# Score priority, a whole-bank output norm, and conditioning products moved to GpSimd and ScalarE in a hybrid decoder trunk

## The chip, the core and the metric

The kernel runs on one core of a Trainium2 chip. A core has five engines with queues of their own: TensorE (PE; its weight loads are listed as PEld), VectorE (DVE), ScalarE (ACT), GpSimd (POOL) and SyncE (SP), which here issues nearly all DMA. Each engine works through its instructions in the order fixed when the kernel was built; semaphores hold an instruction until its operands are there. Matmuls read SBUF and write PSUM, which has eight banks of 128 x 512 float32. The metric is the device time of one execution in microseconds (us), lower is better; the times given are medians over several executions.

## The reference

Two decoder layers on one sequence of 256 tokens of width 1024. A layer has three sub-layers: a half-step SwiGLU FFN, a token mixer, another half-step FFN. Layer 0 mixes with an HGRN2 gated linear recurrence (8 heads, 128 x 128 state, chunks of 64 tokens), layer 1 with a chunked gMLP. Every sub-layer is wrapped in the same way, with shift, scale and gate from a conditioning vector `c`:

```python
cond = jax.nn.silu(c)
mod = (cond @ ada_w[i] + ada_b[i]).reshape(B, 3 * N_SUB, D_MODEL)[:, :, None, :]

def sublayer(x, fn, pre_g, post_g, shift, scale, gate, res_w):
    h = rms_norm(x, pre_g) * (1.0 + scale) + shift
    return x + res_w * gate * rms_norm(fn(h), post_g)
```

The recurrence, per head and chunk (`bb` is the running sum of the log of the forget gate):

```python
o_inter = jnp.einsum('bhtk,bhkv->bhtv', qb * jnp.exp(bb), state)
decay = jnp.exp(jnp.where(causal, diff, -jnp.inf))     # diff = bb[t] - bb[s]
scores = jnp.einsum('bhtk,bhtsk,bhsk->bhts', qb, decay, kb)
o_intra = jnp.einsum('bhts,bhsv->bhtv', scores, vb)
...
o = rms_norm(o, out_norm) * gate        # per head, over 128 values
return o.reshape(B, S, D_MODEL).astype(h.dtype) @ w_out
```

## The kernel before

**Matmuls in three products.** Inputs, weights and results are float32. Each operand is split into a high part in a reduced float32 format and a low part, and a product is made of three matmuls: high x high, high x low, low x high (`mm3`, `mm3f`, `chunk2`; lines 160, 441, 431).

**Weights.** All weights come from HBM once, as a list of blocks of 128 x 2048 float32 in the order of use. A block is brought in as two halves: `cast` (L113) loads a 512 KB half into one of four raw buffers (tile `raw`) and casts it on ScalarE to the high part (L122); `sub` (L129) subtracts on VectorE for the low part (L132). Both parts lie in tiles of a pool of 14 (`wtile`), so at most seven blocks are in SBUF, fewer where the recurrence keeps its own tensors there. `next_block` (L148) hands out the next ready block and makes new ones until `ahead` are in store.

**Conditioning.** The 144 columns of `cond @ ada_w` are not matmuls: each is a 128 x 1024 tile (512 KB) that VectorE multiplies with `cond` and sums along the free axis in one instruction (`ada`, L179; the instruction at L192). Three tiles (`adap`) hold loads in flight; the load of a later one is issued on SyncE's queue when an earlier one is worked off. They are spread over the work as background: `pace(upto, blocks)` sets up to which column the next `blocks` weight blocks bring it, and `wblock` (L141) does so many after each block. The limits per sub-layer are in `bgs` (L1111). `pre_cols` (L197) and `gate_tile` (L212) make the pre-norm columns and the gate row `G` out of them, and first make any column that is still missing.

**Order of the work.** Outside the boundaries a planner orders the instructions of each engine before the run, by priority: a smaller place in the program goes first, when its operands are there by the planner's own estimate. `self.gate` and `hold` add fixed orders to it. Loads on SyncE keep program order.

**Boundary** (`boundary`, L297). Between two sub-layers the order on ScalarE, VectorE and TensorE is written out by hand. There are two token tiles t of 128 and two halves h of 512 columns. For a tile: the last matmuls of the output, `mm(t, h)`; the square and its sum per half (`square`, L235); `gated` (L310), the product with `G`; `half_mean` (L242) and `inv_rms` (L247); `residual` (L251), which adds into `x` and squares the new `x`; `scaled` (L290), the normalised `xn`; then per half four transposes on TensorE (L271), four ScalarE instructions for the high part of `h` (L274), four on VectorE for the same value in float32 (L284) and one difference for the low part (L287). `halves(n)`, `cast` and `sub` between these steps bring in weights for the next sub-layer. The first projection of the next sub-layer (`proj`, L400; matmuls at L412) is laid around the second tile's steps: `p0`, its 48 matmuls for tile 0, is cut after 30 and after 36 of them. In `p0` the 17th to 20th need the low part of half 0, the 21st to 24th that of half 1.

**Recurrence** (`hgrn`, L627). Eight heads in two halves of four (`hb`). `feat` makes features on the partitions, `tok` tokens on the partitions, `gate_f` (L666) the forget gate's logs and exponentials on ScalarE and VectorE. `attn` (L693) is a generator: scores are built in seven levels (64, 32, ... 1); at each, VectorE takes differences (L724, L729), ScalarE the exponential (L80), VectorE a product (L735), TensorE 16 matmuls of 64 columns (L741), and VectorE merges the result of the level before by a mask (L712). At the end the output products (L774, L776) go to PSUM. `zip_steps` alternates a step of `attn` with a step of other matmul work, so that TensorE has something to do. `finish` (L781) is the output norm: eight squares with sums on ScalarE (L787), the reciprocal root, eight scale-and-gate instructions on VectorE (L800), eight transposes (L805), and the split into high and low (L809, L810). For `hb` 0 it runs inside the steps of the second half's `attn`, followed by the output projection of its two pairs of heads (`outs`, L884: two times eight calls of `out_mm`, three matmuls each); for `hb` 1 it stands alone at the end, ahead of the boundary.

## Time and profile before

| | us |
|---|---|
| median of 3 executions | 1200.78 (1199.64 to 1204.22) |
| profiled execution | 1199.71 |
| its span, first to last instruction | 1197.9 |
| TensorE busy | 1144.4 (96%) |
| VectorE busy | 909.9 (76%) |
| ScalarE busy | 663.3 (55%) |
| GpSimd busy | 6.8 (1%) |

The page gives one profiled execution. In a timeline row stand the start, the duration, the engine, the line of the kernel, the operation, output and inputs by the names of their tiles, shapes and count; a bracket at the end is the time that the engine stood idle before it and what ended that. In a row of groups, the number after `x` is the count, then busy time and mean duration in nanoseconds, then idle time before the group with those that ended it. A row of windows gives the busy time of each engine inside a stretch, with counts, the clock granted to TensorE (1.00 is full), the share of time that the DMA engines were busy, and GB/s.

The sub-layers follow one another like this, by the transposes of the boundaries (L271): boundary 0, from the first FFN to the recurrence, around 213 us; boundary 1 around 397 to 413; boundary 2 around 587 to 601; boundary 3, into the gMLP, until about 790; boundary 4 around 1013; the last FFN to the end.

### The profile page before, as it was taken

Reading aid. Unit: us, or ns where it says so; the run is one execution under the profiler, and the core shown is the slowest. Engines: PE = TensorE matmul, PEld = TensorE weight load, DVE = VectorE, ACT = ScalarE, POOL = GpSimd, SP = SyncE. Lnnn points to the kernel's source line nnn. Section 1 sums busy time; section 2 is a strip of 40 time slices with the busy share of each in tenths; the row PEclk is TensorE's granted clock in tenths of the full one; section 3 lists DMA queues with packets and bytes.
Section 4 is the critical chain, followed back from the end, with each engine's and each line's share of the span. In section 5 each row is a group of like instructions: output and inputs, shape, how many; then the busy total and the mean of one; then the engine's idle time right before and its main releaser. Section 6 shows DMA issues by size and latency. Waiting matters only on the chain.

```text
span 1197.9 us, 17119 instructions
## 1 busy us (share of the span) xinstructions
PE 1144.4 (96%) x6518; PEld 997.4 (83%) x6518; DVE 909.9 (76%) x1391; ACT 663.3 (55%) x1054; POOL 6.8 (1%) x16
## 2 busy tenths in 40 slices
PE   7999998898798899999999999999999999999997
PEld 6989997798787688888788888877798997888886
DVE  6987786779867789985589986476898777866642
ACT  6454446668547755555565555553664456645531
POOL 0000000000000000000000000000000000000000
PEclk9999999898899999999999999999999999999999
DMA  9889898296305389986279996426687764766630
GB/s 349 311 315 331 320 351 287 95 327 233 125 35 193 106 293 365 333 307 224 94 261 339 344 334 227 165 80 222 234 316 276 265 201 131 247 216 226 207 106 36
DMA packets 79764, 282.31 MB, mean 236 GB/s; under 512 B 9873, under 2 KB 10561, under 8 KB 79682
## 3 DMA queue, kind: packets, MB, share of 16 engines
q1 hardware_dynamic: 78626, 278.05, 66.0%
q0 software_dynamic: 1056, 3.17, 0.8%
q8 instruction: 51, 0.84, 0.3%
q14 instruction: 31, 0.25, 0.1%
HBM read 280.11 MB, written 1.07 MB: 235 GB/s over the span
## 4 chain that ended last, share of the span: by engine, by line
PE 83%; DVE 8%; DMA 4%; ACT 4%; issue 1%; SPq 0%; DVEq 0%; ACTq 0%
PE ups L437 17%; PE ups L438 9%; PE y L162 8%; PE y L163 8%; PE y L164 8%; PE pps L412 7%; PE ups L557 4%; PE ups L445 4%; PE ups L443 4%; PE ups L444 4%; DVE w L132 2%; PE ab L741 2%; DMA raw<-in_wffn 2%; ACT w L122 1%; PE vps L1003 1%
## 5 line engine op out<-in xcount | busy, mean ns | idle before, releaser
L132 DVE TENSOR_TENSOR w<-raw,w 128x1024 fp32r<-128x1024 f32 x376 | 453.8, 1223 | 113.5 <-ACT w L122 105.5
L122 ACT CAST w<-raw 128x1024 fp32r<-128x1024 f32 x376 | 387.1, 1050 | 167.7 <-DMA raw<-in_wffn 66.0
L437 PE MATMUL ups<-h,w 128*128 128x512 f32 x864 | 302.0, 393 | 0.0
L438 PE MATMUL ups<-h,w 128*128 128x256 f32 x864 | 242.0, 280 | 0.0
L437 PEld LDWEIGHTS ups<-h,w 128*128 128x128 f32 x864 | 161.7, 187 | 36.4
L192 DVE CUSTOM_DVE_ANT_0 ada<-ada,cond 128x1024 f32<-128x1024 f32 x144 | 173.6, 1221 | 21.7 <-DMA ada<-in_ada 21.7
L162 PE MATMUL y<-w,t 128*128 128x512 f32 x448 | 179.7, 402 | 0.0
L163 PE MATMUL y<-w,t 128*128 128x512 f32 x448 | 178.2, 398 | 0.3 <-DVE w L132 0.3
L164 PE MATMUL y<-w,t 128*128 128x512 f32 x448 | 177.7, 397 | 0.0
L438 PEld LDWEIGHTS ups<-h,w 128*128 128x128 f32 x864 | 163.3, 189 | 1.0
L445 PE MATMUL ups<-h,w 128*128 128x256 f32 x416 | 117.9, 283 | 2.1 <-DVE rs_sd L89 1.2
L443 PE MATMUL ups<-h,w 128*128 128x256 f32 x416 | 118.3, 284 | 0.0
L444 PE MATMUL ups<-h,w 128*128 128x256 f32 x416 | 117.7, 283 | 0.0
L412 PE MATMUL pps<-w,h 128*128 128x512 f32 x480 | 115.1, 396 | 0.2 <-DVE h L287 0.2
L412 PEld LDWEIGHTS pps<-w,h 128*128 128x128 f32 x480 | 89.9, 190 | 19.2 <-DVE h L287 0.6
L164 PEld LDWEIGHTS y<-w,t 128*128 128x128 f32 x448 | 84.6, 189 | 20.3
L162 PEld LDWEIGHTS y<-w,t 128*128 128x128 f32 x448 | 84.7, 189 | 18.9
L163 PEld LDWEIGHTS y<-w,t 128*128 128x128 f32 x448 | 84.7, 189 | 18.9 <-DVE w L132 1.4
L445 PEld LDWEIGHTS ups<-h,w 128*128 128x128 f32 x416 | 79.7, 191 | 2.5 <-DVE w L132 2.5
L443 PEld LDWEIGHTS ups<-h,w 128*128 128x128 f32 x416 | 79.7, 192 | 1.0 <-issue 0.2
L444 PEld LDWEIGHTS ups<-h,w 128*128 128x128 f32 x416 | 79.7, 192 | 0.8 <-issue 0.2
L80 ACT ACTIVATE t<-t 128x256 f32<-128x256 f32 (+2 forms) x70 | 36.6, 524 | 50.4 <-DVE t L490 41.7
(196 smaller groups left out, 1327.1 us busy)
## 6 DMA issues: line engine op xcount, KB each, us to landing
raw<-in_wffn SPq DMA_DIRECT2D x264, 512.0 KB, 5.5
ada<-in_ada SPq DMA_DIRECT2D x144, 512.0 KB, 6.7
raw<-in_wgmu SPq DMA_DIRECT2D x48, 512.0 KB, 5.0
raw<-in_whg SPq DMA_DIRECT2D x40, 512.0 KB, 5.2
raw<-in_wgmv SPq DMA_DIRECT2D x24, 512.0 KB, 5.0
G<-gflat POOLq DMA_DIRECT2D x6, 512.0 KB, 5.1
t<-in_gbin SPq DMA_DIRECT2D x6, 256.0 KB, 5.6
x<-in_x SPq DMA_DIRECT2D x2, 512.0 KB, 4.3
```

The source lines that it names most:

```text
L122: self.after(self.nc.scalar.copy(hi[:, sl], raw), self.hold[0])
L132: self.after(self.nc.vector.tensor_sub(lo[:, sl], raw, hi[:, sl]), self.hold[1])
L162: self.paced(mm(ps, l[0], r[0], start=start, stop=False))
L163: mm(ps, l[0], r[1], start=False, stop=False)
L164: mm(ps, l[1], r[0], start=False, stop=stop)
L192: self.after(nc.vector.tensor_tensor_reduce(t, t, self.cond, 1.0, 0.0, ALU.mult, ALU.add, self.mod[i // 24][:, i % 24:i % 24 + 1]), self.h ...
L412: lambda g=g, i=i, j=j, kc=kc, w=w: mm(res[g][t], h2[:, i, t, kc, :], w, start=kc + i + j == 0, stop=i == 1 and kc == KC - 1)))
L437: self.paced(mm(ps, u[0], self.h2[:, :, :, kc, :], start=kc == 0, stop=False))
L438: self.last = mm(ps[:, 1, :], u[1], self.h2[:, 0, :, kc, :], start=False, stop=kc == KC - 1)
L443: self.paced(mm(o, u[0], h[0], start=start, stop=False))
L444: mm(o, u[0], h[1], start=False, stop=False)
L445: self.last = mm(o, u[1], h[0], start=False, stop=stop)
```

## The change

- **Conditioning in the recurrence** (`ada`): while `self.pooled` is set, a product is a `tensor_mul` on GpSimd, in place, and its sum a ScalarE `activation` (Copy) with an accumulated output. It is set in `hgrn` from the start to just before its end.
- **Pace**: the first FFN's limit goes from 46 to 40 columns, the recurrence (limit 64) spreads its own over 14 blocks, not 9, and the third FFN's limit goes from 118 to 120.
- **Priority**: each step of `attn` is built 400 places ahead in the planner's priority.
- **Output norm**: squares of a whole bank into SBUF, sums and the gating product on VectorE by whole banks, then eight scalings of 128 x 128. At the end of the recurrence it is written out by hand in the boundary's region, opened earlier for that; the output projection of the second pair of heads (24 matmuls, `fill`) is taken out of the alternation and laid between its steps.
- **Boundaries**: `half_mean` of the residual comes after both halves; for half 1 of tile 0 the float32 value of `h` is made on ScalarE ahead of the residual, and its difference on VectorE after it; the projection is built after that; `p0` is cut at 35 and 41; the weight half in the midst of this goes to the end of the boundary. Boundary 1 has its own numbers of weight halves.
- **gMLP**: the gate row is made at unit 8 of 12, not before the units; three small constants are loaded at the start of the kernel.

```diff
@@ ada
-            self.after(nc.vector.tensor_tensor_reduce(t, t, self.cond, 1.0, 0.0, ALU.mult, ALU.add,
-                                                      self.mod[i // 24][:, i % 24:i % 24 + 1]), self.hold[1])
+            m = self.mod[i // 24][:, i % 24:i % 24 + 1]
+            if self.pooled:
+                nc.gpsimd.tensor_mul(t, t, self.cond)
+                self.after(nc.scalar.activation(t, t, AF.Copy, accum_out=m), self.hold[0])
+            else:
+                self.after(nc.vector.tensor_tensor_reduce(t, t, self.cond, 1.0, 0.0, ALU.mult, ALU.add, m),
+                           self.hold[1])
@@ residual
                 self.square(self.x[t][:, hs], st[0], h)
-                if h == 0:
-                    self.half_mean(st)
+        if st is not None:
+            self.half_mean(st)
@@ h_low becomes h_full and h_low
+    def h_full(self, h, pa, cols, scalar=False):
...
+            if scalar:
+                nc.scalar.activation(hf[:, ks], pa[:, ks], AF.Identity, bias=sh[:, kc:kc + 1], scale=A[:, kc:kc + 1])
+            else:
+                nc.vector.tensor_scalar(hf[:, ks], pa[:, ks], A[:, kc:kc + 1], sh[:, kc:kc + 1],
+                                        op0=ALU.mult, op1=ALU.add)
+        return hf
@@ boundary
+    def boundary(self, y, G, mm, cols, table, plan=(4, 2, 0, 0)):
...
-        self.halves(4)
+        self.halves(plan[0])
...
-        self.halves(2)
+        self.halves(plan[1])
...
+        for _ in range(plan[2]):
+            self.cast()
         self.residual(0, yg, r, sx)
+        for _ in range(plan[2]):
+            self.sub()
...
-        self.h_low(0, 0, pa0, cols)
-        self.h_low(0, 1, pa1, cols)
-        w = [[self.ready.pop(0) for _ in range(2)] for _ in range(2)]
-        self.res, go = self.proj(w)
+        self.h_low(0, 0, self.h_full(0, pa0, cols))
         sq(1, 1, sy1)
         gated(1, 1, yg1)
         r = self.inv_rms(sy1)
-        self.cast()
+        for _ in range(plan[3]):
+            self.cast()
+        hf = self.h_full(1, pa1, cols, scalar=True)
         self.residual(1, yg1, r, sx1)
-        self.sub()
+        for _ in range(plan[3]):
+            self.sub()
+        self.h_low(0, 1, hf)
+        w = [[self.ready.pop(0) for _ in range(2)] for _ in range(2)]
+        self.res, go = self.proj(w)
...
-        do(p0[0:30])
+        do(p0[0:35])
         pa0, _ = self.h_high(1, 0, xn, cols)
-        do(p0[30:36])
+        do(p0[35:41])
         pa1, act = self.h_high(1, 1, xn, cols)
-        do(p0[36:])
-        self.h_low(1, 0, pa0, cols)
-        dve = self.h_low(1, 1, pa1, cols)
+        do(p0[41:])
+        self.h_low(1, 0, self.h_full(0, pa0, cols))
+        dve = self.h_low(1, 1, self.h_full(1, pa1, cols))
+        self.halves(1)
@@ hgrn
-        self.pace(bg, 9)
+        self.pace(bg, 14)
+        self.pooled = True
...
+        def attn(hb, bank, res):
+            gen = attn_steps(hb, bank, res)
+            while True:
+                with tc.high_priority(offset=400):
+                    if next(gen, gen) is gen:
+                        return
+                yield
...
+        def stats(hb, ops, sqrt):
...
+            for u in range(2):
+                sqs.append(self.t2().rearrange("p (i v) -> p i v", i=4))
+                nc.scalar.activation(sqs[u], ops[u].rearrange("p t h v -> p (t h) v"), AF.Square)
+            def gated(u):
+                c0 = 2 * (2 * hb + u) * P
+                nc.vector.tensor_mul(og[:, 512 * u:512 * u + 512].rearrange("p (t c) -> p t c", t=NT),
+                                     ops[u].rearrange("p t h v -> p t (h v)"), gg[:, :, c0:c0 + 2 * P])
+            for u in range(2):
+                nc.vector.reduce_sum(ss[:, 4 * u:4 * u + 4], sqs[u], axis=mybir.AxisListType.X)
+                if u == 0:
+                    gated(0)
             nc.vector.tensor_scalar(ss, ss, 1.0 / P, EPS, op0=ALU.mult, op1=ALU.add)
             if sqrt:
                 self.tact(ss, ss, AF.Sqrt)
+                self.cast()
+                gated(1)
                 nc.vector.reciprocal(r, ss)
...
+        def turn(hb, u, og, r):
...
+                nc.vector.tensor_scalar(on[:, i, :], on[:, i, :], r[:, 4 * u + i:4 * u + i + 1], None, op0=ALU.mult)
...
-        finish(1, ops[1], True)
+        self.ahead, self.pooled = 0, False
+        fill = products(1)
         wos = [nb()]
         self.ahead = 1
         wos.append(nb())
+        self.open()
+        self.gate = state["ops"]
+        for op in fill[:5]:
+            op()
+        og, r = stats(1, ops[1], True)
+        ps = [turn(1, 0, og, r)]
+        fill[5]()
+        ps.append(turn(1, 1, og, r))
+        self.sub()
+        for op in fill[6:]:
+            op()
+        for u in range(2):
+            split(1, u, ps[u])
         nxt(y, G, self.out_last(y, oTs[2:], wos))
@@ gmlp: G = G_fn() moves from before the units to
+            if u == 8:
+                G = G_fn()
@@ run
-        bgs = {"ffn0": 46, "hg": 64, "ffn1": 92, "ffn2": 118, "gm": 138, "ffn3": 144}
+        bgs = {"ffn0": 40, "hg": 64, "ffn1": 92, "ffn2": 120, "gm": 138, "ffn3": 144}
...
+                    self.boundary(y, G, mm, st["cols"], tables[subs[s + 1][0]], (2, 1, 1, 1) if s == 1 else (4, 2, 0, 0))
```

More of the change, by code (lines that the diff above doesn't have):

```diff
@@ L775, in attn @@
                                              start=True, stop=False)
-                        nc.tensor.matmul(ops[:, t, hd, :], St[:, hl * S + t * P:hl * S + (t + 1) * P],
-                                         v[:, t, c0:c0 + P], start=t == 0, stop=True)
+                        state["ops"] = nc.tensor.matmul(
+                            ops[:, t, hd, :], St[:, hl * S + t * P:hl * S + (t + 1) * P],
+                            v[:, t, c0:c0 + P], start=t == 0, stop=True)
                 res.append(ops)
@@ L779, in attn @@
             yield
-        def finish(hb, ops, sqrt=False):
+        def attn(hb, bank, res):
[6 more added lines that the diff above has]
+        def stats(hb, ops, sqrt):
             ss = self.tiny.tile([P, 8], F32, tag="ss8", name="ss8")
-            o4 = [o.rearrange("p t h v -> p (t h) v") for o in ops]
+            r = self.tiny.tile([P, 8], F32, tag="r8", name="r8")
+            og, sqs = self.t4(), []
@@ L784, in finish @@
             for u in range(2):
-                for i in range(4):
-                    junk = self.scr.tile([P, 512], BF16, tag="junka", name="junka")
-                    nc.scalar.activation(junk[:, 0:P], o4[u][:, i, :], AF.Square, accum_out=ss[:, 4 * u + i:4 * u + i + 1])
+                sqs.append(self.t2().rearrange("p (i v) -> p i v", i=4))
[4 more added lines that the diff above has]
+                                     ops[u].rearrange("p t h v -> p t (h v)"), gg[:, :, c0:c0 + 2 * P])
@@ L793, in finish @@
             else:
+                gated(1)
                 self.rsqrt(r, ss)
[L795 to L811 removed]
@@ new lines, in stats @@
+            return og, r
+        def turn(hb, u, og, r):
+            on = og[:, 512 * u:512 * u + 512].rearrange("p (i v) -> p i v", i=4)
+            for i in range(4):
+                nc.vector.tensor_scalar(on[:, i, :], on[:, i, :], r[:, 4 * u + i:4 * u + i + 1], None, op0=ALU.mult)
+            ps = self.acc.tile([P, 512], F32, tag="acc", name="ots")
+            for i in range(4):
+                c0 = (i % 2) * S + (i // 2) * P
+                nc.tensor.transpose(ps[:, c0:c0 + P], on[:, i, :], self.ident)
+            return ps
@@ L813, in hgrn, with split @@
+        def split(hb, u, ps):
+            pair = 2 * hb + u
+            if not oall:
+                oall.extend([self.wtile() for _ in range(2)])
+            oT = [o[:, 512 * pair:512 * pair + 512] for o in oall]
+            nc.scalar.activation(oT[0], ps, AF.Copy, scale=self.onorm)
+            nc.vector.scalar_tensor_tensor(oT[1], ps, self.onorm, oT[0], op0=ALU.mult, op1=ALU.subtract)
+            oTs.append([o.rearrange("p (h s) -> p h s", h=2) for o in oT])
         ybank = {"i": 0}
@@ L1102, in run @@
         self.blocks, self.blk, self.ready, self.ahead = [], 0, [], 0
-        self.half, self.casts, self.hold = None, [], (None, None)
+        self.half, self.casts, self.hold, self.pooled = None, [], (None, None), False
         for src, n, k in ((d["wffn"][0], 2048, 33), (d["whg"], 2048, 20), (d["wffn"][1], 2048, 33),
```

63 lines of the change are left out of this document (21 added, 42 removed).

## The prediction

> **What bounds the kernel now.** I read the page first, then the order of time on TensorE for places where it stands still, then busy time by stretch, and last what the other engines did ahead of each stop.
>
> ```profile
> PE 1144.4 (96%) x6518; PEld 997.4 (83%) x6518; DVE 909.9 (76%) x1391; ACT 663.3 (55%) x1054; POOL 6.8 (1%) x16
> PE 83%; DVE 8%; DMA 4%; ACT 4%; issue 1%; SPq 0%; DVEq 0%; ACTq 0%
> ```
>
> TensorE is busy in 1144.4 of 1197.9 us and carries 83% of the chain that ended last. Nothing in the diff removes a matmul, so all that can be won is TensorE's idle time, some 53 us, and the slow clock that follows a long stop. The timeline of TensorE shows the stops (the bracket is the idle time and what ended it):
>
> ```profile
> 213.51 0.47 PE L271 MATMUL npa<-ident,xn 128*128 128x128 f32 x1 [8.09 <-DVE be L242]
> 289.17 0.45 PE L741 MATMUL ab<-t 128*128 128x64 f32 x1 [5.09 <-ACT L L679]
> 314.67 0.45 PE L741 MATMUL ab<-t 128*128 128x64 f32 x1 [6.64 <-DVE t L735]
> 382.51 0.90 PE L805 MATMUL ots<-ident,t 128*128 128x128 f32 x3 [4.95 <-DVE t L800]
> 397.48 0.33 PE L271 MATMUL npa<-ident,xn 128*128 128x128 f32 x1 [1.56 <-DVE be L242]
> 409.07 0.33 PE L271 MATMUL npa<-ident,xn 128*128 128x128 f32 x1 [2.41 <-DVE xn L293]
> 598.80 0.33 PE L271 MATMUL npa<-ident,xn 128*128 128x128 f32 x1 [1.57 <-DVE xn L293]
> 787.40 0.33 PE L271 MATMUL npa<-ident,xn 128*128 128x128 f32 x1 [1.98 <-DVE xn L293]
> 837.79 0.27 PE L219 MATMUL gps<-ident,gate 128*8 128x128 f32 x1 [1.15 <-DVE w L924]
> 838.93 0.50 PE L163 MATMUL pps<-w,h 128*128 128x512 f32 x1 [0.86 <-DVE w L132]
> 854.16 0.39 PE L445 MATMUL ups<-h,w 128*128 128x256 f32 x1 [0.93 <-DVE w L132]
> 1012.76 0.33 PE L271 MATMUL npa<-ident,xn 128*128 128x128 f32 x1 [1.56 <-DVE xn L293]
> ```
>
> L271 is the transpose in a boundary between two sub-layers (five of them: I count from 0), L741 the recurrence's scores, L805 its output's transposes, L219 and L163 lie in the gMLP. After a long stop the clock is down as well; the 16 score matmuls of one level, once after the stop at 289 and once in full flow (columns: stretch, its length, TensorE busy, weight loads busy, granted clock, DMA share, GB/s):
>
> ```profile
> 289.10:292.90 3.80, 3.65 (x16) 3.49 (x16) 0.50 0.29 116
> 298.60:300.60 2.00, 1.89 (x16) 1.82 (x16) 1.00 0.03 8
> ```
>
> 3.65 against 1.89: a stop of 5 us or more costs 1.76 us on top. Those under 2 us show no such loss: I price them at their length.
>
> **Boundary 0 (the FFN into the recurrence).** The wait at 213.51 names a DVE row, but the delay starts on ScalarE:
>
> ```profile
> 204.65 1.05 ACT L122 CAST w<-raw 128x1024 fp32r<-128x1024 f32 x1 [1.93 <-DMA raw<-in_whg]
> 206.22 1.05 ACT L122 CAST w<-raw 128x1024 fp32r<-128x1024 f32 x1 [0.52 <-DMA raw<-in_whg]
> 207.17 0.59 ACT L235 ACTIVATE junka<-y 128x512 bf16<-128x512 f32 x1
> ```
>
> Two weight casts, written into the order ahead of the square of the second half, wait for their loads. TensorE's last matmul before the stop ended at 213.51 - 8.09 = 205.4; the 27 between (18 of mm(1,0), 9 of mm(1,1)) at 0.23 us each put the end of mm(0,1) at about 199. The square at 207.17 is 8 us late, and the chain behind it, 6.3 us to 213.51, is shorter than the cover. What makes the loads late is the first FFN's traffic:
>
> ```profile
> 150.00:180.00 30.00, 30.00 (x207) 27.72 (x206) 25.02 (x35) 12.63 (x16) 1.22 (x2) 1.00 0.97 351
> ...
> ada<-in_ada SPq DMA_DIRECT2D x144, 512.0 KB, 6.7
> ```
>
> With a DMA share of 0.97 at 351 GB/s the stream is DMA's. The limit of conditioning products in this FFN goes from 46 to 40: six loads of 512 KB fewer, 3.15 MB / 351 GB/s = 9.0 us of stream. That is about the lateness, so the stop should nearly go: of 8.09 + 1.76 = 9.85 I take 7.5. Bounds: 0 (the stream holds back elsewhere, in the four raw buffers) and 9.85. If the loads come, next is the chain itself.
>
> **Boundaries 2, 3 and 4.** ScalarE and VectorE in boundary 2 ahead of the stop at 598.80, and the matmuls that cover it:
>
> ```profile
> 590.24 2.46 PE L412 MATMUL pps<-w,h 128*128 128x512 f32 x10
> ...
> 591.63 1.04 ACT L122 CAST w<-raw 128x1024 fp32r<-128x1024 f32 x1
> ...
> 591.65 1.37 DVE L284 TENSOR_SCALAR hf<-npa,A,shift 128x128 f32<-128x128 f32 x4
> 593.66 0.68 DVE L310 TENSOR_TENSOR yg<-y,G 128x512 f32<-128x512 f32 x1
> 596.00 0.15 DVE L242 TENSOR_SCALAR be<-s 128x1 f32<-128x1 f32 x1 [0.79 <-ACT junka L235]
> ```
>
> The product L310 could run at 591.6, when ScalarE's square is over, but stands behind four scalings (1.37) and a difference (0.69). The change gives those four to ScalarE, in the place of the cast (1.04), and puts the difference behind the residual: 2.06 us won. The half mean no longer stands between the two halves of the residual: 0.79 won. So xn comes near 596, not 598.8, while the cover grows from 30 to 35 matmuls, (2.46 - 0.39) / 9 = 0.23 us each, to 598.4. The stop goes. The price: the difference, now behind the residual, is needed by the 21st matmul, at 590.24 + 20 x 0.23 = 594.9; I work it out to end at 594.6. The moved cast and difference lie under the next 48 matmuls (11 us). Term: 1.57 + 1.98 + 1.56 = 5.1; bounds 3 (0.7 us late three times) and 5.1.
>
> **Boundary 1 (out of the recurrence).** Same edits, but two casts and two differences stay inside. For the first tile the half mean saves 0.8 of the 1.56. For the second, a cast (1.04) ahead of the scalings and a 1.22 difference (the same tile as VectorE's L132) ahead of the moved one make that about 3.3 us late for the 21st matmul, for the 2.41 now. Net 0, bounds -1 and +2.
>
> **The recurrence's inside (222 to 377).** Columns: TensorE, weight loads, DVE, ACT and POOL busy, clock, DMA share, GB/s.
>
> ```profile
> 222.00:283.00 61.00, 61.00 (x438) 57.57 (x437) 51.84 (x86) 42.74 (x69) 0.00 (x0) 1.00 0.66 234
> 283.00:308.00 25.00, 19.91 (x125) 18.90 (x124) 21.73 (x37) 19.26 (x37) 0.00 (x0) 0.80 0.59 207
> 308.00:335.00 27.00, 19.95 (x111) 17.90 (x111) 19.69 (x30) 12.67 (x21) 0.52 (x1) 0.81 0.36 117
> 335.00:377.00 42.00, 42.00 (x279) 38.12 (x280) 33.43 (x61) 28.00 (x61) 0.55 (x1) 1.00 0.26 85
> ...
> L122 ACT CAST w<-raw 128x1024 fp32r<-128x1024 f32 x34 | 34.6, 1048 | 12.9 <-DMA raw<-in_whg 9.5 <-PE tps L163 2.0 <-PE fps L444 1.3
> L132 DVE TENSOR_TENSOR w<-raw,w 128x1024 fp32r<-128x1024 f32 x34 | 40.8, 1225 | 7.0 <-ACT w L122 6.9
> L192 DVE CUSTOM_DVE_ANT_0 ada<-ada,cond 128x1024 f32<-128x1024 f32 x18 | 21.5, 1223 | 0.8 <-DMA ada<-in_ada 0.8
> L192 DVE DVE_READ_ACCUMULATOR2_ANT mod<- 128x1 f32 x18 | 1.6, 86 | 0.0
> L787 ACT ACTIVATE junka<-ab 128x128 bf16<-128x128 f32 x14 | 3.9, 277 | 3.6 <-PE ab L776 3.3
> L787 ACT ACTIVATION_READ_ACCUMULATOR junka<-ab 128x1 f32 x14 | 2.7, 196 | 0.0
> ...
> SPq L57 <- DVE mod L192: 65.5, 11, 24.2
> ```
>
> The two stops, 5.09 and 6.64, come where the scores' chain stands behind other work on VectorE and ScalarE; 400 steps of priority for it attack just that. Both with their clock are 5.09 + 6.64 + 2 x 1.76 = 15.25 us. Against it stands the moved load. The fence shows four stretches, five groups of these 155 us, and SyncE's longest waits (in all, times, longest). VectorE was busy 126.7 us and loses 18 x (1.223 + 0.086) = 23.6: 103. ScalarE, 102.7, gets 24 sums of 1.048 (the cast's row, same elements) + 0.196 (the accumulator's read) = 29.9, and gives back 8 x 0.473 for two squares of 0.6, 2.6: 130. TensorE needs 142.9 less its slow-clock 3.5, 139. So ScalarE goes from 74% to 93% of what TensorE needs, and in strict order it cannot hide it all. Six conditioning loads more come, 24 over 14 blocks for 18 over 9. SyncE waited 65.5 us for a conditioning tile to come free, with weight loads queued behind; that tile now comes free after GpSimd and ScalarE. And 24 matmuls of the output (5.6 us) leave the second half's scores for the end of the stage, where VectorE would be at (33.4 + 2) of 36.4 us. I take half of 15.25: 7.5. Bounds: 15.25, and nothing won with ScalarE's rest in the way; the loss beyond is a rival.
>
> GpSimd computes nothing in the trace. The multiplication's price lies above the 1.22 of VectorE's row; 155 / 24 = 6.5 us is where GpSimd itself sets the stage. I take a price near the first, and free, since POOL shows only 0.52 and 0.55 us here: the gate's two transfers, which now stand behind products on that queue but are not used before boundary 1. What is new is a wait: each sum on ScalarE waits for its product, and behind it in ScalarE's order stand weight casts and the scores' exponentials, for which TensorE waits.
>
> **The stage's end.** At 382.51 TensorE waits for the output norm. Its scalings will be 128x128 out of SBUF, for which the trace has one row of four times the size:
>
> ```profile
> 598.26 0.49 DVE L293 TENSOR_SCALAR xn<-x,r 128x512 f32<-128x512 f32 x1
> ```
>
> New: 15 of the moved matmuls (3.5 us) run in its shadow. The chain: square 0.59 (as at 207.17); per bank a sum and a product, four instructions of 0.68 (L310's row; a free-axis sum has none of its own, and the quoted VectorE rows of 128x512 lie between 0.49 and 0.68); mean and reciprocal 0.15 each (as L242); four scalings between 0.12 (a quarter of 0.49) and 0.34 (L284's 1.37 / 4, from PSUM): 1.0. Some 4.6, so 1.1 stays. Won: 4.95 - 1.1, and most of the clock's 1.76: 5. Bounds 0 (the casts now written ahead of the squares wait for weights) and 6.7.
>
> **The gMLP.** The gate's two products held VectorE up:
>
> ```profile
> 834.61 1.23 DVE L192 CUSTOM_DVE_ANT_0 ada<-ada,cond 128x1024 f32<-128x1024 f32 x1 [4.81 <-DMA ada<-in_ada]
> ```
>
> They move into the FFN before (limit 118 to 120), the gate to unit 8, three small loads to the start. The stops of 1.15, 0.86 and 0.93 and some clock: 4; bounds 2 and 5.
>
> **Sum**: 7.5 + 5.1 + 0 + 7.5 + 5 + 4 = 29.1. The profiled execution took 1199.7 (span 1197.9), the median is 1.1 higher: 1200.8 - 29.1 = 1171.7.
>
> **The rivals.**
> (a) ScalarE becomes the recurrence's bound, or the priority moves nothing since weights, not scores, are late there: the inside gives 0, 1179. For it: 93%. Against: the sums are the least urgent work.
> (b) Boundary 0 stays late, the loads held by the raw buffers: 1179. Against: the 0.97.
> (c) Slower: while GpSimd multiplies, VectorE's instructions with two operands in SBUF are held up, p us each time. VectorE needs 103 + 24p for the stage: the 139 are passed at p = 1.5, today's 155 at 2.2, and at 3.1 it eats the 21.6 us won elsewhere. With p = 3.5 it is 187, 32 more than today, 1211. The trace has no GpSimd arithmetic to tell; against it, only part of VectorE's work has two such operands.
>
> The Trainium skill, "SBUF — State Buffer", section "Who interferes with whom", says just this: a VectorE instruction with two SBUF inputs and a GpSimd one that reads SBUF exclude each other, the later one blocked until the first is done. "GPSIMD Engine Reference", "Performance versus the Vector engine", has 4497 ns for 2048 elements of a two-input op; half, 2.25 us, is my estimate from it. By it VectorE would need 157 us, the inside would lose 2 us for the 7.5 won, and the time be 1181. No row here shows either.
>
> **Chances.** Forecast 0.47 (1164 to 1178), everything recovered 0.04 (1157), (a) 0.14, (b) 0.10; (c) 0.07 at p about 2.3 (158 us, so 3 lost where 7.5 were to be won: 1182), 0.07 near 3.1, no change, and 0.11 above 3.4. About 0.5%, 6 us, is what a measurement tells from no change. Faster 0.82, same 0.07, slower 0.11. The range runs from all bounds on the good side, 1157, to 1197, (c) at p near 3; outside it some 0.17.
>
> **What would show it.** Boundary 0: the casts before the second square end before 199, no stop over 2 us. Boundaries 2 to 4: no stop at L271. Recurrence: no stop over 3 us at the scores, sums of some 1.2 us on ScalarE, VectorE's L132 still 1.22. Wrong it is if L132 or the score differences stretch wherever POOL is busy, if ScalarE is full with TensorE waiting, or if stops near 20 matmuls into a projection take the place of those removed.

## The result and the profile after

The changed kernel takes 1207.43 us in the median of 18 runs (1201.44 to 1211.96); the kernel before took 1200.75 us beside it (18 runs, 1198.55 to 1205.65). The ratio is 1.0054, 95% interval 1.0039 to 1.0070: slower by about half a per cent, where 1172 us had been forecast. The profiled execution of the changed kernel has a span of 1203.5 us, 5.6 more than before.

By the first transposes of each boundary the span splits into six parts. Before, they stood at 213.5, 397.5, 587.3, 775.5 and 1001.2 us; after, at 207.1, 411.0, 600.9, 787.3 and 1008.2.

| part | before, us | after, us | difference | forecast |
|---|---|---|---|---|
| start to boundary 0 | 213.5 | 207.1 | -6.4 | -7.5 |
| recurrence, boundary 0 to 1 | 184.0 | 203.9 | +19.9 | -13.3 (inside 7.5, end 5, first tile of boundary 1 0.8) |
| boundary 1 to 2 | 189.8 | 189.9 | +0.1 | about +1 |
| boundary 2 to 3 | 188.2 | 186.4 | -1.8 | -1.6 |
| boundary 3 to 4, with the gMLP | 225.8 | 220.9 | -4.9 | -6.0 |
| boundary 4 to the end | 196.7 | 195.3 | -1.4 | -1.6 |

Five of the six parts came out within about 1.2 us of the forecast. The recurrence took it all back and more. The stretch of the recurrence before, and then after (columns: stretch, its length, busy time of TensorE, weight loads, VectorE, ScalarE and GpSimd, granted clock, DMA share, GB/s):

```profile
213.50:397.50 184.00, 165.34 (x1032) 149.95 (x1032) 147.41 (x255) 120.03 (x224) 1.08 (x2) 0.92 0.48 167
```

```profile
207.10:411.00 203.90, 172.08 (x1031) 154.78 (x1032) 154.90 (x222) 140.77 (x247) 64.72 (x24) 0.88 0.48 164
```

TensorE stands still for 31.8 us, not 18.7, and does the same matmuls in 6.7 us more at a lower clock (0.88 for 0.92). VectorE has 33 instructions fewer in it than before and is nevertheless busy for 7.5 us more. The timeline of TensorE after, the stops that answer to those of the prediction:

```profile
207.10 0.66 PE L276 MATMUL npa<-ident,xn 128*128 128x128 f32 x4 [1.93 <-DVE be L247]
266.44 0.79 PE L724 MATMUL ab<-w 128*128 128x128 f32 x2 [7.62 <-ACT w L80]
330.26 0.94 PE L724 MATMUL ab<-w 128*128 128x128 f32 x6 [3.90 <-DVE t L725]
370.29 1.08 PE L851 MATMUL ots<-ident,t 128*128 128x128 f32 x4 [11.27 <-DVE t L847]
396.99 0.92 PE L851 MATMUL ots<-ident,t 128*128 128x128 f32 x4 [2.65 <-DVE t L847]
420.44 0.80 PE L434 MATMUL pps<-w,h 128*128 128x512 f32 x1 [3.08 <-DVE h L298]
919.19 0.71 PE L1065 MATMUL vps<-w 128*128 128x128 f32 x4 [1.73 <-DVE t L1072]
```

Line numbers are those of the changed kernel: L276 is the boundary's transpose, L724 the scores of the level of single positions, which needs all gates of a half, L851 the output's transposes, L434 the projection, L1065 a gMLP product. The two stops at the scores (5.09 and 6.64) are gone. In their place stand 7.62 and 3.90 ahead of a half's first scores and, largest of all, 11.27 ahead of the output transposes of the first half, where before there was none. Three smaller stops, of 2.10, 1.64 and 1.18 us, are new in the recurrence too. From boundary 2 to 3 TensorE does not stop at all; it is busy for the whole stretch:

```profile
600.90:787.30 186.40, 186.40 (x963) 158.13 (x962) 151.50 (x223) 109.36 (x180) 1.08 (x2) 1.00 0.77 274
```

What is new in the recurrence shows in the groups of instructions between 207 and 411 us of the changed kernel (columns: group, count, busy us, mean ns of one, idle time ahead of it and what ended it):

```profile
L194 POOL TENSOR_TENSOR ada<-ada,cond 128x1024 f32<-128x1024 f32 x22 | 63.6, 2903 | 113.6 <-DMA ada<-in_ada 101.5 <-ACT t L80 8.8 <-ACT L L694 2.8
L195 ACT ACTIVATE ada<-ada 128x1024 f32<-128x1024 f32 x24 | 25.3, 1055 | 12.7 <-POOL ada L194 12.7
L752 DVE TENSOR_TENSOR t<-w 128x512 f32<-128x512 f32 x12 | 14.7, 1225 | 0.0
L747 DVE TENSOR_TENSOR t<-w 128x512 f32<-128x512 f32 x12 | 11.4, 948 | 1.3 <-PE ab L784 1.3
```

GpSimd takes 2.9 us for one product, not a price near VectorE's 1.22. The score differences L747 and L752, one form and one size, take 0.95 and 1.23 us in the mean; undisturbed they take 0.69 (a row below). Where the longest stop comes from is seen in the timeline of GpSimd and, under it, of VectorE:

```profile
352.23 11.69 POOL L194 TENSOR_TENSOR ada<-ada,cond 128x1024 f32<-128x1024 f32 x4 [7.08 <-DMA ada<-in_ada]
...
353.26 0.68 DVE L829 TENSOR_REDUCE ss<-t 128x4 f32<-128x512 f32 x1
353.85 0.68 DVE L825 TENSOR_TENSOR t<-ab,w 128x512 f32<-128x512 f32 x1
354.45 1.70 DVE L747 TENSOR_TENSOR t<-w 128x512 f32<-128x512 f32 x1
356.07 2.88 DVE L752 TENSOR_TENSOR t<-w 128x512 f32<-128x512 f32 x1
358.88 2.83 DVE L747 TENSOR_TENSOR t<-w 128x512 f32<-128x512 f32 x1
361.63 2.82 DVE L752 TENSOR_TENSOR t<-w 128x512 f32<-128x512 f32 x1
364.38 0.68 DVE L758 TENSOR_TENSOR t<-t,w 128x512 f32<-128x512 f32 x1
```

Four products run on GpSimd without a break, from 352.23 to 363.92. In that time the four differences, which read both operands from SBUF, take 1.70, 2.88, 2.83 and 2.82 us instead of 0.69 each: 7.5 us lost. The sum L829, with one operand, and the gating product L825, with one of its two from PSUM, keep their 0.68. The rest of the first half's output norm stands behind the four on VectorE, and TensorE has nothing else left. Such rows are not only large ones. At the start of the stage a sum of 128 x 8 elements (L635) is held up by a product for 2.33 us, and ScalarE, with two weight casts and the gate's logarithms queued behind, waits for it on the way to the stop of 7.62:

```profile
257.89 0.22 ACT L80 ACTIVATE lb_s<-lb_s 128x16 f32<-128x16 f32 x1 [3.05 <-DVE lb_s L635]
```

In all, 14 VectorE instructions of the stage are stretched, by 26.4 us together (each row's length less that of the same form undisturbed); all of them have both operands in SBUF and fall under a GpSimd product. (The expectation of e1 says 18 and some 25 us. Four merges L735 of 1.32 us are not counted here, since they take as long in e1, where GpSimd has no products.) Conversely the longest product, 6.56 us, lies under a run of such VectorE rows.

### The profile page after: what moved, and what is told of

Read it like the earlier page. It is cut to its first block, busy times and chain, and to the rows that moved or that the text cites. A ratio compares the mean times of both kernels' runs of the same rounds, so it can differ in the third digit from the quotient of the medians.

```text
span 1203.5 us, 17134 instructions
## 1 busy us (share of the span) xinstructions
PE 1148.1 (95%) x6518; PEld 1000.7 (83%) x6518; DVE 906.0 (75%) x1331; ACT 691.0 (57%) x1094; POOL 75.3 (6%) x40
## 4 chain that ended last, share of the span: by engine, by line
PE 79%; DVE 8%; DMA 5%; ACT 5%; issue 2%; POOL 0%; SPq 0%; DVEq 0%; ACTq 0%; POOLq 0%
PE ups L459 16%; PE ups L460 9%; PE pps L434 8%; PE y L164 8%; PE y L163 8%; PE y L162 8%; PE ups L579 4%; PE ups L465 3%; PE ups L467 3%; PE ups L466 3%; PE ab L764 2%; DVE w L132 2%; DMA ada<-in_ada 2%; ACT w L122 2%; PE pps L162 1%
## 5 line engine op out<-in xcount | busy, mean ns | idle before, releaser
L197 DVE CUSTOM_DVE_ANT_0 ada<-ada,cond 128x1024 f32<-128x1024 f32 x120 | 145.3, 1219 | 18.5 <-DMA ada<-in_ada 18.4
L434 PE MATMUL pps<-w,h 128*128 128x512 f32 x480 | 115.6, 397 | 3.1 <-DVE h L298 3.1
L434 PEld LDWEIGHTS pps<-w,h 128*128 128x128 f32 x480 | 90.3, 191 | 22.3 <-DVE h L298 3.5
L194 POOL TENSOR_TENSOR ada<-ada,cond 128x1024 f32<-128x1024 f32 x24 | 68.3, 2861 | 123.0 <-DMA ada<-in_ada 101.5
```

The source lines that it names most:

```text
L197: self.after(nc.vector.tensor_tensor_reduce(t, t, self.cond, 1.0, 0.0, ALU.mult, ALU.add, m), self.hold[1])
L434: lambda g=g, i=i, j=j, kc=kc, w=w: mm(res[g][t], h2[:, i, t, kc, :], w, start=kc + i + j == 0, stop=i == 1 and kc == KC - 1)))
```

## The experiments

Three theories are tried: L, that VectorE and GpSimd exclude each other when both read SBUF; S, that ScalarE's queue is what costs, since sums wait for GpSimd and weight casts and exponentials stand behind them; P, that the priority puts score matmuls in front of work that was ready. The ratio is to the kernel before, run beside, with its 95% interval.

**e1_vector_products: the products back on VectorE.** All else as changed.

```diff
-        self.pooled = True
+        self.pooled = False
```

> The changed kernel, but the recurrence's 24 conditioning products stay single instructions on VectorE; priority, norm and boundaries as changed. Theory L (GpSimd and VectorE exclude each other; 18 VectorE instructions were stretched by some 25 us in all in the changed trace) and theory S (ScalarE's queue: 24 sums of 1.2 us, 12.7 us of waiting for GpSimd, weight casts behind them) both expect the recurrence, now 204 us from boundary 0 to boundary 1, to fall to 175 to 185 us and the time to 1180 to 1190. Theory P (the priority put the scores' first matmuls, L724, and the output's transposes ahead of work that was ready) expects little: the stops at these lines stay, 1200 to 1207.

1191.15 us, ratio 0.9926 (0.9912 to 0.9941). The products on GpSimd and the sums on ScalarE cost some 15 us against VectorE doing both. That is just above what L and S expected and well below P's range; P's stop at L724 is gone, but the one at the output's transposes (L851) has grown from 11.27 to 15.59 us.

**e2_no_priority: the scores without priority.**

```diff
-                with tc.high_priority(offset=400):
+                if True:
```

> The changed kernel without the 400 places of priority for the scores. Theory P expects the stop of 7.6 us at the first score matmuls (L724) to go and the time to fall by 8 us or more, to 1199 or less. Theories L and S expect the stretched VectorE instructions and the late casts as before and a time within 5 us of 1207.

1201.21 us, ratio 1.0018 (1.0000 to 1.0036): 4 to 6 us better than the change, and the two intervals (from 1.0039 up for the change) do not meet. The stop of 7.62 us at L724 is gone, as theory P expected, but the time fell by less than its 8 us. The priority is not a gain here.

**e3_neither: both undone.**

> The changed kernel with the products on VectorE and without the priority. If the two do not interact, its gain over the changed kernel is the sum of those of the two kernels that undo one each. Theory P: below the one with products on VectorE alone by 8 us or more. Theories L and S: the same as that or slower, since the scores lose their place: 1183 to 1195.

1181.94 us, ratio 0.985 (0.9832 to 0.9869). What is left of the change is faster than the kernel before by 1.5%. Against e1 it shows that the priority costs 9 us also where no GpSimd is at work, as theory P had it. Most of it lies at the output norm of the first half; TensorE's row in e1, and then in e3:

```profile
353.87 1.30 PE L851 MATMUL ots<-ident,t 128*128 128x128 f32 x5 [15.59 <-DVE t L847]
```

```profile
346.39 1.94 PE L851 MATMUL ots<-ident,t 128*128 128x128 f32 x8 [8.84 <-DVE t L847]
```

**e4_write_only: GpSimd writes, but reads nothing.** The same number of GpSimd instructions, in a kernel whose TensorE, VectorE and ScalarE run the same instructions in the same order as the changed one.

```diff
-                nc.gpsimd.tensor_mul(t, t, self.cond)
+                nc.gpsimd.memset(t, 0.0)
```

> The changed kernel in the same order of instructions, but GpSimd's 24 instructions write zeros into the conditioning tile and read nothing (the multiplication by the conditioning vector is left out for these columns, so their sums are 0). ScalarE's sums and their wait for GpSimd stay. Theory L (the exclusion is on reads): no VectorE instruction of two SBUF operands is stretched any more, the 11.3 us stop at the output's transposes falls below 4 us, the time falls by 10 to 18 us, to 1190 to 1197. Theory S: the sums still stand in ScalarE's order, time within 4 us of 1207 unless the shorter GpSimd instruction also shortens the waits (then some 5 us). Theory P: the 7.6 us stop at L724 stays.

1180.35 us, ratio 0.983 (0.9809 to 0.985): 27 us less than the change, by one instruction, and more than the 10 to 18 that L expected. The stops at the two places where the change lost most, 7.62 and 11.27 us there, are short:

```profile
261.16 0.71 PE L724 MATMUL ab<-w 128*128 128x128 f32 x4 [1.35 <-ACT w L80]
346.88 0.87 PE L851 MATMUL ots<-ident,t 128*128 128x128 f32 x3 [4.74 <-DVE t L847]
```

What the reads do shows at one place that the two have in common: the gate's first two VectorE rows L708, which start 0.37 us after a GpSimd instruction. First the changed kernel, then e4:

```profile
266.58 2.37 POOL L194 TENSOR_TENSOR ada<-ada,cond 128x1024 f32<-128x1024 f32 x1 [2.93 <-DMA ada<-in_ada]
...
266.95 2.68 DVE L708 SCALAR_TENSOR_TENSOR w<-w,loglb,L 128x256 f32<-128x256 f32 x2 [3.82 <-ACT L L80]
```

```profile
261.29 0.95 POOL L194 MEMSET ada<- 128x1024 f32 x1 [2.08 <-DMA ada<-in_ada]
...
261.66 0.88 DVE L708 SCALAR_TENSOR_TENSOR w<-w,loglb,L 128x256 f32<-128x256 f32 x2 [3.83 <-ACT L L80]
```

2.68 us for the two against 0.88. No VectorE row of e4's stage is stretched; its differences keep their length:

```profile
L747 DVE TENSOR_TENSOR t<-w 128x512 f32<-128x512 f32 x12 | 8.2, 686 | 3.8 <-PE ab L764 3.5 <-PE ab L784 0.2
```

But the fill is also shorter, 0.95 us for 2.9, so the sums come earlier too. The next three runs part the two.

**e5_long_write: three fills.** As long as a product, and no read.

```diff
-                nc.gpsimd.tensor_mul(t, t, self.cond)
+                [nc.gpsimd.memset(t, float(z)) for z in (2, 1, 0)]
```

> In place of the multiplication GpSimd writes the conditioning tile three times over (three fills of about 0.95 us each, as the run that only writes showed for one, so about 2.9 us, which is as long as the multiplication took, 2.37 to 3.3 us). It leaves out the multiplication by the conditioning vector for the recurrence's 24 columns, whose sums become 0. Theory L (VectorE and GpSimd exclude each other on reads): GpSimd is busy as long as in the changed kernel but reads nothing, so no VectorE row stretches, and the time stays near that of the one fill, 1180 to 1185 us. Theory S (what costs is that the product, and with it the sum on ScalarE and the casts behind it, comes 2 us later): 1195 us or more, with VectorE's rows at their usual lengths.

1191.11 us, ratio 0.9934 (0.9901 to 0.9968), between the two theories. The runs scatter from 1183.84 to 1195.87 (the profile is of the fastest), and the planner moved part of the order with the three instructions. No row with two SBUF operands is stretched. What its 11 us over e4 are, length or order, is not told by it.

**e6_one_read: GpSimd reads one operand.** Same order as the change.

```diff
-                nc.gpsimd.tensor_mul(t, t, self.cond)
+                nc.gpsimd.tensor_scalar(t, t, 1.0, None, op0=ALU.mult)
```

> In place of the multiplication of two tiles GpSimd multiplies the conditioning tile by the constant 1: one operand read from SBUF and not two. It leaves out the multiplication by the conditioning vector for the recurrence's 24 columns. Theory L, for any read of GpSimd's: VectorE's rows with two SBUF operands still stretch to the end of the GpSimd row, and the time is above 1190 us, by how much depends on how long the row is (it has not been seen; at 2.4 us it would be near the changed kernel's 1207, at 1.2 us near 1190). Rival L2 (only GpSimd's second operand collides): no row stretches, 1180 to 1185 us.

1193.87 us, ratio 0.9959 (0.9945 to 0.9973). GpSimd is no faster than in the change (3.0 us a piece in the mean, shortest 2.77), so the sums are as late, and yet some 12 us are won. Rows are still held up, but for less; the same place again:

```profile
263.14 2.77 POOL L194 TENSOR_SCALAR ada<-ada 128x1024 f32<-128x1024 f32 x1 [0.69 <-DMA ada<-in_ada]
...
263.49 1.36 DVE L708 SCALAR_TENSOR_TENSOR w<-w,loglb,L 128x256 f32<-128x256 f32 x2 [3.62 <-ACT L L80]
```

1.36 us, between 0.88 and 2.68: the first of the two went on some 0.85 us after GpSimd's start, not at its end. The stage's 12 stretched rows lose 8 us together, against 26.4. My expectation that they would stretch to the GpSimd row's end was wrong. Since order and length of GpSimd's work are as in the change, this pair is the cleanest price of a read: 18 us less of stretch, some 12 us less of time.

**e14_sum_first: the sum ahead of the product.** GpSimd reads as before, but no sum waits for it.

```diff
-                nc.gpsimd.tensor_mul(t, t, self.cond)
                 self.after(nc.scalar.activation(t, t, AF.Copy, accum_out=m), self.hold[0])
+                nc.gpsimd.tensor_mul(t, t, self.cond)
```

> The changed kernel with its two instructions in the other order: ScalarE sums the conditioning tile as it was loaded, and GpSimd multiplies it afterwards, so that no sum waits for GpSimd. It leaves the conditioning vector out of the recurrence's 24 sums; GpSimd reads and multiplies as before. Theory L (the reads themselves, through VectorE's stretched rows): the rows still stretch, 1198 to 1207 us. Theory S (a sum that comes 2 us later, and the casts behind it): 1181 to 1188 us. From the runs so far (1180 without reads, 1191 without reads but with long writes, 1194 with one operand read, 1207 with two) about two thirds of the 27 us would be L's, which puts this run at 1196 to 1200.

1207.93 us, ratio 1.0064 (1.0041 to 1.0086): as slow as the change. In the changed kernel ScalarE's longest waits for GpSimd were the first row (in all, times, longest); in this run no ScalarE row waits for GpSimd, and GpSimd waits for ScalarE (second fence):

```profile
ACT ada L195 <- POOL ada L194: 12.7, 6, 3.2
```

```profile
POOL ada L195 <- ACT ada L194: 131.0, 12, 67.7
```

The stretched rows are still there, some 30 us of them; here an addition of 128 x 8 elements:

```profile
256.88 2.46 POOL L195 TENSOR_TENSOR ada<-ada,cond 128x1024 f32<-128x1024 f32 x1 [2.75 <-ACT ada L194]
...
256.97 2.39 DVE L221 TENSOR_TENSOR gate<-mod,adab 128x8 f32<-128x8 f32 x1
```

With reads and without the wait 1208, without reads 1180: with e4 and e6, whose order is the change's, L is shown, and S as the main cause falls. The size of L is not told by this run: the planner moved its order in places, and SyncE's loads stand for 87.4 us at conditioning tiles that are not free yet, for 49.9 in the change. I had put this run at 1196 to 1200, too low.

**e15_write_no_priority: e4 without the scores' priority.**

> The run in which GpSimd only writes (1180.4 us), without the priority of the scores. It leaves out the multiplication by the conditioning vector for the recurrence's 24 columns. If the priority costs the same here as with the products on VectorE (1191.2 against 1181.9) or on GpSimd (1207.4 against 1201.2), 1171 to 1174 us. If it costs only because conditioning products or held-up rows fill VectorE, and gains where VectorE is free, as the prediction had it, 1183 to 1188 us.

1177.70 us, ratio 0.9827 (0.9802 to 0.9852), for e4's 0.983: no difference that these intervals tell, and neither expectation met. Where neither conditioning products nor held-up rows weigh on VectorE the priority costs little or nothing, and gains nothing. The stretch from boundary 0 to boundary 1 of e4 and of this run:

```profile
208.20:386.80 178.60, 165.25 (x1032) 148.89 (x1032) 128.70 (x222) 140.46 (x247) 22.05 (x24) 0.93 0.54 187
```

```profile
206.60:381.30 174.70, 163.40 (x1031) 148.82 (x1031) 127.68 (x221) 139.76 (x247) 22.07 (x24) 0.94 0.54 191
```

ScalarE carries the 24 sums in both and is busy for 140 us, as in the changed kernel (140.77), with the stage 25 to 29 us shorter. So ScalarE's load was not the cause.

**e8_scores_and_norm_first: e1 with the first half's output norm ahead of the scores.**

```diff
-            og, r = stats(0, ops[0], False)
-            for u in range(2):
-                split(0, u, turn(0, u, og, r))
+            with tc.high_priority(offset=800):
+                og, r = stats(0, ops[0], False)
+                for u in range(2): split(0, u, turn(0, u, og, r))
```

> The conditioning products on VectorE as in the first of these runs (1191.2 us), the scores with their priority, and the output norm of the first half (statistics, scalings, transposes, split) with a higher one. Theory N: what the priority costs (1191.2 against 1181.9) lies in one place, the stop of 15.6 us ahead of the first half's output transposes, since the norm's chain on VectorE stands behind scores and eight conditioning products of 1.22 us; ahead of them, the stop falls below 5 us and the time to 1178 to 1183 us. Theory P (the score matmuls take TensorE's order from work that was ready, all over the stage): the stop goes but comes back at the scores, 1188 to 1192 us.

1188.38 us, ratio 0.9909 (0.9892 to 0.9925). The stop of 15.59 shrank to 5.03, as theory N had it, but the time stayed where the other theory put it, for a reason neither had: a new stop ahead of the last products. (Five conditioning products fell into e1's stop, not the eight that the expectation names.) TensorE, and what ScalarE did in the meantime:

```profile
337.02 1.30 PE L851 MATMUL ots<-ident,t 128*128 128x128 f32 x5 [5.03 <-DVE t L847]
379.39 0.79 PE L162 MATMUL y<-w 128*128 128x512 f32 x1 [12.39 <-ACT w L859]
...
366.21 1.05 ACT L122 CAST w<-raw 128x1024 fp32r<-128x1024 f32 x1 [3.49 <-DMA raw<-in_whg]
...
375.38 1.04 ACT L122 CAST w<-raw 128x1024 fp32r<-128x1024 f32 x1 [2.00 <-DMA raw<-in_wffn]
...
378.66 0.68 ACT L859 ACTIVATE w<-ots,onorm 128x512 fp32r<-128x512 f32 x1
```

The transposes were done at 365.6, but the split L859 stood behind seven weight casts that waited for their loads.

**e10_scores_norm_queue and e11_b1_queue: conditioning loads on another queue.** In e8 and in e9 (below), all 144 conditioning loads are issued by GpSimd's queue.

```diff
-                self.load(t, self.d["ada"][j])
+                self.tc.keep_in_program_order(nc.gpsimd.dma_start(t, self.d["ada"][j]))
```

> The run with priority for scores and first norm (1188.4 us), whose conditioning tiles are now loaded by GpSimd's DMA queue and no longer by SyncE's. Theory W: in that run the stop of 12.4 us ahead of the last products of the output comes from weight casts on ScalarE that wait for loads, and these were issued late, since SyncE's queue stood 22.8 us at a conditioning load that waited for its tile. With a queue of their own the weights come in time, the stop falls to under 4 us and the time to 1178 to 1181 us. Rival: the transfers themselves are the limit there (DMA share 0.85 in that stretch): 1186 to 1190 us.

> The run with priority for the first norm and the earlier difference (1180.5 us), its conditioning tiles loaded by GpSimd's DMA queue. No stop of over 1 us on TensorE names a weight there, so the queue should change little: 1178 to 1182 us. If weights were what sets the whole stage's pace, behind the stops at scores and norm, it gains as much as the run above, 1170 to 1175 us.

1226.69 us (ratio 1.0232, 1.0204 to 1.0261) and 1222.76 us (1.0198, 1.0162 to 1.0233): both 38 to 42 us slower, and neither expectation holds. Most of it arises outside the recurrence, which takes 183.7 and 182.4 us in them, for 185.2 in e8 and 180.3 in e9. The edit was too wide, since it moved the loads of every stage. In e10 a stop of 9.29 us behind a waiting cast remains at the stage's end, so that SyncE's queue was the cause in e8 is not shown and stays open.

**e9_norm_and_b1: e3 with the norm ahead, and in boundary 1 the difference ahead of the weight difference.**

```diff
         self.residual(1, yg1, r, sx1)
+        self.h_low(0, 1, hf)
         for _ in range(plan[3]):
             self.sub()
-        self.h_low(0, 1, hf)
```

> Both undone (no priority for the scores, the products on VectorE: 1181.9 us), with two edits of its own: priority for the output norm of the first half, and in boundary 1 the second tile's difference ahead of the weight difference and not behind it. Theory N: the stop of 8.8 us ahead of the first half's output transposes falls below 4 us, and the stop of 3.07 us in boundary 1 by one weight difference, 1.22 us, to about 1.85: 1181.9 - 5 - 1.2 = 1175 to 1177 us. Rival: the norm only takes VectorE's time from the scores, which are late instead: 1180 to 1182 us.

**e13_b1_plan: e9 with no cast in that place.**

```diff
-... (2, 1, 1, 1) if s == 1 ...
+... (3, 1, 1, 0) if s == 1 ...
```

> The run with priority for the first norm and the earlier difference (1180.5 us), with no cast and weight difference inside the second half of boundary 1, and one more pair ahead of its first matmuls. By the prediction's step for boundary 1 (a cast of 1.04 us ahead of ScalarE's scalings makes the difference late for the 21st matmul) the stop there falls from 1.94 us to about 0.9 us and the time by 1 us, to 1179.5 us; if the pair is late in its new place, a stop of 1 to 2 us shows at boundary 1's first transposes.

1180.47 us (ratio 0.9846, 0.9824 to 0.9868) and 1181.83 us (0.9851, 0.9819 to 0.9883): both as e3, within the intervals. The stop in boundary 1 obeys step by step, 3.07 in e3, then e9 and e13:

```profile
397.24 0.50 PE L434 MATMUL pps<-w,h 128*128 128x512 f32 x1 [1.94 <-DVE h L298]
```

```profile
397.26 0.50 PE L434 MATMUL pps<-w,h 128*128 128x512 f32 x1 [1.01 <-DVE h L298]
```

But in e9 the norm's stop of 8.84 only changed place: 3.40 us appear at the scores at 349 and the stop at the stage's end grows from 1.47 to 3.48. Of e9's expected 6 us none is seen in the time.

**e12_limit_46: e3 with the first FFN's limit back at 46** (and so 18 products in the recurrence, not 24).

```diff
-... "ffn0": 40, ...
+... "ffn0": 46, ...
```

> Both undone (1181.9 us), and the first FFN's limit of conditioning products back from 40 to 46, so that the recurrence has 18 again and not 24. By the prediction's step for boundary 0 (six loads of 512 KB, 9 us of stream, make the two casts ahead of the second square late) the stop at boundary 0, 1.9 us, comes back to about 8 us and the time rises by 6, to 1188, less up to 6 x 1.3 us that VectorE saves in the recurrence. Rival: the half mean's new place and the recurrence's own loads carry it, and the stop stays near 2 us: 1179 to 1183 us.

1187.14 us, ratio 0.9898 (0.987 to 0.9925), some 5 us slower than e3. The stop at boundary 0 is back, 7.06 us for e3's 1.91, with the new half mean in place:

```profile
211.92 0.91 PE L276 MATMUL npa<-ident,xn 128*128 128x128 f32 x3 [7.06 <-DVE be L247]
```

## Why the prediction was wrong, and where it was right

**The failed step is the GpSimd product in the recurrence's inside**: "I take a price near the first, and free." It took 2.37 us at the least and 2.9 in the mean, and it was not free. With a fill of 0.95 us in its place the kernel is 27 us faster (1207.4 against 1180.4), and the first scores and the first half's norm wait 1.35 and 4.74 us for 7.62 and 11.27. Part of this is the reads: e6, in the same order and with GpSimd's rows as long, reads one operand less and is some 12 us faster. How the rest divides between its remaining reads (8 us of stretch) and the longer instruction stays open; e5, with long fills and no reads, leaves up to 11 us for length and order. Held-up VectorE rows are the mechanism of rival (c), which I gave a quarter of the chances, and the prediction's own sign of it, score differences that stretch where GpSimd is busy, is in the trace. The pricing of (c) failed too. I counted VectorE's total, 103 + 24p, against what TensorE needs, and by that nothing is lost below p = 1.5. Measured, p is 26.4 / 24 = 1.1, and VectorE is busy in 154.9 of the stage's 203.9 us; yet the stage is 25 us longer than in e4. A held-up row costs time not only when its engine is full, but already when it lies in the chain that TensorE waits for next: the gate's sums ahead of the first scores, the differences ahead of the first half's norm.

The Trainium skill, "SBUF — State Buffer", section "Who interferes with whom", has the rule: two SBUF inputs on VectorE contend with a GpSimd instruction that reads SBUF, not with one that only writes. The trace agrees with both halves, 2.68 and 0.88 us for the same two rows. The sum made by that page of the Trainium skill gave 1181, since the same total stood behind it; the rule was right and the price I hung on it was not.

**The priority, for which half of 15.25 us was counted, gains nothing.** The stops of 5.09 and 6.64 at the scores are gone, as forecast, but mostly not by the priority: in e3, without it, one of 3.00 is all that is left of them (which of the other edits took the rest away is not shown).

```profile
279.33 0.87 PE L764 MATMUL ab<-t 128*128 128x64 f32 x3 [3.00 <-ACT t L80]
```

And the term asked only what the scores wait for, and not what their VectorE work would stand in front of: the first half's norm, which had no stop before, waits 8.84 us without the priority (e3) and 15.59 with it (e1). Moving the norm forward won nothing that the times tell: in e9 its stop came back at the scores and at the stage's end, in e8 a new one rose behind weight casts. e1 against e3 has it at 9 us lost with conditioning on VectorE, e2 against the change at 4 to 6 on GpSimd, e4 against e15 at nothing measurable. That scores and norm wait for the same VectorE work, whichever goes first, fits these pairs but is argued, not shown.

**Rival (a)**, ScalarE as the bound, is out: 140 us busy in stages of 174.7 and 203.9 us alike.

**Boundary 0**: 7.5 forecast, 6.4 measured; the stop went from 8.09 to 1.93. The six loads explain most of it, as said: giving them back costs 5.2 us of stop. The two casts did not end before 199 us, as I had asked; ScalarE's rows of the changed kernel, the casts and the second square:

```profile
199.59 2.18 ACT L122 CAST w<-raw 128x1024 fp32r<-128x1024 f32 x2 [0.50 <-DMA raw<-in_whg]
201.68 0.58 ACT L240 ACTIVATE junka<-y 128x512 bf16<-128x512 f32 x1
```

They end at 201.8, 5.5 us sooner than before and 2.8 past the 199, which fits the stop of 1.93 that is left.

**Boundaries 2 to 4**: right. No stop is left there, for 5.1 us forecast. **Boundary 1**: right, with 3.08 for "about 3.3", and e9 and e13 take out its two causes at 1.1 and 0.9 us. **The stage's end**: 2.65 us are left of 4.95, where 1.1 was worked out; the 4.6 us chain was short, as rows of others stood between. **gMLP**: with boundary 3's 1.98 taken off the part's 4.9, 2.9 for 4; a new stop of 1.73 us at L1065 is more than the difference.

**Without the failed steps** (neither GpSimd's reads nor the priority, e15, which leaves the multiplication out) the ratio is 0.9827, 20.8 us of the forecast 29.1. The working version of this kind is e3, with 1.5% under the kernel before; e9 and e13 are its equals.

## What to carry to other kernels

Before work is moved to GpSimd, list the VectorE instructions with two SBUF operands in the chains that TensorE waits for, and price each at the full GpSimd product; a total of VectorE's time did not show the loss here. Moving work forward by priority must be priced by what it is put in front of, on every engine that it uses. A change of many parts can hide 1.5% behind two bad parts: undo the parts one at a time.

## What the runs showed of the hardware that was not expected

- How long a VectorE row is held does not depend on its size: sums of 128 x 8 elements took 2.33 us (L635, the change) and 2.39 us (L221, e14) under a product, 0.17 us undisturbed; they lost some 2.2 us, as the differences of 128 x 512 did.
- A tensor_scalar with one operand, in and out of SBUF, was held up as well, by reads and by writes: the mean L832 of 128 x 8 elements, 0.16 us elsewhere, took 2.30 us under a product in e14 and 1.29 under the fills in e5. The reduction L829, with one operand too, was not. The Trainium skill, "SBUF — State Buffer", section "Who interferes with whom", has a mode of two ports that tensor_scalar can enter and a reduction can not; the rows agree with that. VectorE's rows in e14 and e5:

```profile
365.30 2.30 DVE L832 TENSOR_SCALAR ss<-ss 128x8 f32<-128x8 f32 x1
```

```profile
342.69 1.29 DVE L832 TENSOR_SCALAR ss<-ss 128x8 f32<-128x8 f32 x1
```

- The hold depends on what GpSimd reads. Under two operands VectorE's row went on only when the GpSimd row was over: the sum L635 ended at 257.85 us, the product at 257.83. Under one, of 2.77 us and no faster, VectorE went on about 0.85 us after its start. The same page of the Trainium skill has the later one blocked for the whole instruction; for one operand this run does not bear that out.
- A product of 128 x 1024 float32 on GpSimd takes 2.37 us at the least, and 6.56 under a run of VectorE rows with two SBUF operands; the estimate of 2.25 from "GPSIMD Engine Reference", section "Performance versus the Vector engine", in the Trainium skill was near the first. A fill of the same size takes 0.95.
- A shorter stop than the 5 us of the prediction already costs TensorE its clock. In e3, after the stop of 3.00 us, the 16 score matmuls of one level took 3.65 us, for 1.89 in full flow in the kernel before (columns: stretch, its length, TensorE busy, granted clock, DMA share, GB/s):

```profile
279.30:283.10 3.80, 3.65 (x16) 0.50 0.67 227
```

- 512 KB loads issued by GpSimd's queue instead of SyncE's, 144 of them, made the kernel 38 to 42 us slower. Why is open.
